# A hybrid decoder step on one core: four tiles' rows turned by VectorE instead of TensorE, and one fold of GLA's first chunk moved ahead

## The chip, the cores and the metric

The kernel runs on one core of one Trainium2 chip. The metric is the device time of one launch in microseconds, the median of several runs. The core has five engines that run side by side, each through its own instructions in order: TensorE (PE in the profile; its weight loads are PEld), VectorE (DVE), ScalarE (ACT), GpSimd (POOL) and SyncE (SP, which issues nearly all DMAs). They wait for each other by semaphores.

## The reference

One inference step of one layer. 2048 prompt tokens and 64 sampled tokens (8 sequences of 8) go through a mixer with two head groups, an output projection, and a squared-ReLU MLP, each with an RMSNorm before and after and a residual:

```python
h = rms_norm(x, g_mix_pre)
proj = h @ w_in                      # split into q, k, v and the GLA parts
attn = sliding-window attention with sinks (window 128)
o    = gated linear attention (GLA), chunked, then rms_norm and silu gate
mix = concat(attn, gla_out) @ w_out
x = x + rms_norm(mix, g_mix_post)
h = rms_norm(x, g_ffn_pre)
u = relu(h @ w_up)
f = (u * u) @ w_down
x = x + rms_norm(f, g_ffn_post)
```

All is f32. The model width is 1024, the MLP's 4096. The new keys, values and GLA states are returned as well.

## The kernel before, in words

The prompt's 2048 rows are 16 tiles of 128 (0 to 15), the 64 sampled rows are tile 16 (`NB`). f32 products are made as three products of split operands: a high part (a ScalarE copy into a rounded type) and a low part (a VectorE subtraction). The stages follow each other: input projection and attention, GLA, the out stage, then the MLP in two halves of 1024 rows (`sb` 0 and 1), each an up stage and a down stage. The MLP's products use a seven-product scheme over 2x2 blocks (Strassen's), so the normalized rows of a tile and of its partner four tiles later (0 and 4, 8 and 12) are combined into seven operands `H[1]` to `H[7]`.

**Out stage.** Tiles go in the order `B_ORDER`: 0, 4, 1, 5, 2, 6, 3, 7, 16, 8, 12, 9, 13, 10, 14, 11, 15. For each tile the 48 products of `out_projecting` (L1581) are issued, and then `residual` of the tile two places earlier in that order. For a tile, `residual` does in steps (a generator; each `yield` ends a step):

- `mixed`: ScalarE squares both halves of the product (`bjunk<-out`, L1696), VectorE adds the sums (`bssq`, L1697), POOL takes the power -0.5 (L221), VectorE scales the product (`x<-out`, L1703; the tile named `x` there is `x1` in the code) and adds the residual (`bx<-x,bx`, L1704).
- ScalarE squares the sum (`bjunk<-bx`, L1809), VectorE and POOL form the factor, VectorE normalizes (`x<-bx,bssq,gpre`, L1812). This is called the tile's norm below.
- PE turns the 128x1024 rows in eight 128x128 transposes into two PSUM banks (`xnT`, L1822), and ScalarE copies each bank into `ht` (L1831), a tile of seven slots. The first of a pair fills slots 0 and 1, the second slots 6 and 2.
- For the second of a pair, VectorE makes the other slots by four subtractions (`ht<-ht`, L1840). Slots 0 and 1 are stored to DRAM after the first tile (L1836), slots 2 to 6 after the second (L1845).

The rows of the next products are loaded by SP (`mt<-mix_d`, L1534) when PE has done the products that used the same buffer, and split by ScalarE (L231) and VectorE (L232). For the last products of the stage the up stage's first operands are split between them (`t`, `H<-hraw`, `s`, recorded at L143, as all that goes through the in-order helper is).

**The second half's rows.** `h_d[1]` holds the seven operands of rows 1024 to 2047. In the first half's down stage `fetch_h` (L1857) loads each operand in two parts (`hraw<-h_d`, 512 KB each), and `load_h` (L1899, L1900) splits it. There the products run in units of 12 (14 with the sampled rows), and their operand pairs (`o0s`, `o0t`, `o1s`, `o1t`, L2253 and L2254) are made two units ahead.

**GLA's first chunk.** `gla(0)` issues its vector work in program order and, at each `yield`, lets a number of steps of other work in. These numbers are `G_FIRST_FILL`. The fill at this place is the projection of the sampled rows (`gproj`, PE), which ends for each column block in a folding of its two halves into `gp_s` (ScalarE copy, VectorE add). The fourth number stands ahead of the six `weighted_queries` (`XQ<-dec,qz`), the fifth behind them. PE can take the next column block only when the fold has emptied its bank.

The build orders each engine's instructions by a compile-time scheduler, which follows program order loosely; so an edit also moves neighbours.

Of the kernel before, what the change touches and what calls it, by code (L numbers as in the profile page):

```python
# [12 lines left out]
F32 = mybir.dt.float32  # L13
F32R = mybir.dt.float32r
U8 = mybir.dt.uint8
AF = mybir.ActivationFunctionType
# [5 lines left out]
P = 128  # L22
# [24 lines left out]
NSB = 2  # L47
# [27 lines left out]
G_ORDER = (0, 1, 2, 3)  # L75
G_FILL = (3, 5, 6, 10, 8, 2, 14, 4, 4, 10, 8, 20)
G_LAST_FILL = (2, 4, 5, 7, 6, 2, 11, 2, 3, 7, 6, 15)
G_FIRST_FILL = (6, 6, 6, 10, 10, 4, 16, 4, 4, 5, 5, 20)
S_WAIT = (2, 6)
WO_PARTS = ((), (0, 1, 2), (3, 4, 5), (6, 7))  # L80
B_ORDER = (*(j + b for j in range(4) for b in (0, 4)), NB, *(j + b for j in range(4) for b in (8, 12)))
# [72 lines left out]
def hybrid_step_kernel(ctx: ExitStack, tc: tile.TileContext, I, O):  # L154
# [1636 lines left out]
    with tc.issue_after(placing[0].ins):  # L1791
        res_x[B_ORDER[1]], loaded = load_x(B_ORDER[1])

    late_copies, latest_store = [], []

    def residual(i, banks, tensor=nc.tensor, scalar=nc.scalar, vector=nc.vector):

        n = rows(i)
        x = res_x.pop(i, None) or load_x(i)[0]
        ssq = sp.tile([P, 48], F32, tag="ssq", name=f"bssq_{i}", bufs=2)  # L1800
        junk = sp.tile([P, D], mybir.dt.bfloat16, tag="junk", name=f"bjunk_{i}", bufs=1)
        x1 = R["x"].tile([P, D], F32, tag="x1", name=f"x1_{i}", bufs=2)
        if i == NB:
            banks = [folded(x1[:NS, c * 512 : (c + 1) * 512], p_) for c, p_ in enumerate(banks)]
        if banks:
            g = g_mix if tensor is nc.tensor else [gpost[:, c * 512 : (c + 1) * 512] for c in range(2)]
            yield from mixed(i, banks, x, x1, junk, ssq, g, sp, scalar, vector)
        rs = ssq[:, 3:5]
        scalar.activation(junk[:n], x[:n], AF.Square, accum_out=ssq[:n, 2:3])  # L1809
        yield  # L1810
        rsqrt_mean(sp, rs[:n, 1:2], ssq[:n, 2:3], n, D, vector=vector)
        vector.scalar_tensor_tensor(x1[:n], x[:n], rs[:n, 1:2], gpre[:n], op0=ALU.mult, op1=ALU.mult)  # L1812
        yield
        sb, j, second = i // 8, i % 4, i % 8 >= 4
        q = slice(j * P, (j + 1) * P)
        if i < NB and not second and i:
            sums[sb, j] = sums[sb, j - 1] if sb and j else ht_place(f"ht_{i}")
        for h in range(2):
            kk = slice(h * 4, h * 4 + 4)
            pt = (bank([P, 512], "ce"[h], f"xnT_{i}_{h}") if te is tensor else next_bank("cdce", f"xnT_{i}_{h}")).rearrange("p (k t) -> p k t", k=4)  # L1820
            for k in range(4):
                tensor.transpose(pt[:, k, :n], x1[:n, (h * 4 + k) * P : (h * 4 + k + 1) * P], ident[:n, :n])  # L1822
            if i == NB:
                split_copy(xsT[:, kk, :NS], xsT[:, kk, NS:], pt[:, :, :NS], vector)
                continue
            ht = sums[sb, j]
            copy = (ht[:, (6, 2)[h] if second else h], pt, AF.Copy)
            if i == B_ORDER[-2]:
                late_copies.append(copy)
            else:  # L1830
                scalar.activation(*copy)  # L1831
# [6 lines left out]
        yield  # L1838
        for out, a, b in ((4, 6, 0), (6, 2, 6), (5, 2, 4), (3, 1, 5)):
            vector.tensor_tensor(ht[:, out], ht[:, a], ht[:, b], op=ALU.subtract)  # L1840
            if out == 6 and i == B_ORDER[-1]:
                yield
        if i == B_ORDER[-3]:
            yield
        latest_store[:] = [nc.sync.dma_start(h_d[sb][:, 2:, :, q], ht[:, 2:])]  # L1845

    h_raws = {}

    def fetch_h(sb, p, home="h"):
        h_raws[p] = []  # L1850
        for k in range(0, KT // 2, 2):
            if isinstance(home, tuple):
# [4 lines left out]
            fetched = nc.sync.dma_start(raw, h_d[sb][:, p - 1, k : k + 2])  # L1857
# [62 lines left out]
    for n, i in enumerate(B_ORDER[2:]):  # L1920
# [227 lines left out]
    def opening(p, taken, ahead, add):  # L2148

        if p == 1:  # L2150
            for copy in late_copies:
                ac.activation(*copy)
            nc.sync.dma_start(h_d[1][:, :2, :, 3 * P :], sums[1, 3][:, :2])
            taken(p)
            next(last_rows)
            loaded = placing[0]
# [473 lines left out]
```

## Time and profile before

| what | value |
|---|---|
| median of 3 runs | 2136.56 us (2136.18 to 2137.39) |
| profiled execution | 2138.09 us, its span 2136.3 us |
| granted TensorE clock | 0.999 of full speed |
| DMA | 421.73 MB, 197 GB/s on average |

The profiled execution is one run by itself, 1.5 us above the median. Its span is the time from the first to the last instruction. In rows by time the columns are start (us from the span's start), length (us), engine, line of the kernel, operation, result and sources, partitions x elements, and count; a bracket gives idle time of the engine just before and what ended it. Several like instructions in one row overlap a little, so start to start is shorter than the sum of their lengths.

### The profile page before, as it was taken

What the parts mean: (1) busy time and instruction counts of PE and PEld (TensorE: products, weight loads), DVE (VectorE), ACT (ScalarE), POOL (GpSimd) and SP (SyncE); (2) the same over time, 40 slices, a digit from 0 to 9 for tenths busy, and PEclk for the clock granted to TensorE, in tenths of its full rate; (3) what the DMA queues carried; (4) which work ended last, traced back from release to release, by engine and by line L of the source; (5) the groups of instructions that cost most, each with busy time, mean ns of one, the idle gap of its engine ahead of it and who ended that gap; (6) DMA issues with size and microseconds to landing.
All of it is one profiled execution on the core that took longest, in us unless ns stands there. A gap on an engine that the chain in (4) does not pass through costs nothing.

```text
span 2136.3 us, 34547 instructions
## 1 busy us (share of the span) xinstructions
PE 2124.3 (99%) x11828; PEld 1839.5 (86%) x11828; DVE 1528.0 (72%) x3209; ACT 1209.9 (57%) x2690; POOL 223.0 (10%) x393
## 2 busy tenths in 40 slices
PE   9999999999999999999999999999999999999998
PEld 9999999999998888888888888888888888888887
DVE  7999878788886667888887655557766666555576
ACT  7999867566764445655554644344454444544454
POOL 4676510000001110000000000000000000000000
PEclk9999999999999999999999999999999999999999
DMA  7444334546667668687876777668544443766685
GB/s 244 150 148 142 113 100 93 128 113 166 189 201 265 202 208 269 223 274 260 277 257 230 262 236 223 209 197 281 185 149 158 157 158 134 253 204 197 190 273 179
DMA packets 309324, 421.73 MB, mean 197 GB/s; under 512 B 80204, under 2 KB 213308, under 8 KB 305036
## 3 DMA queue, kind: packets, MB, share of 16 engines
q1 hardware_dynamic: 308988, 419.26, 61.2%
q8 instruction: 93, 1.52, 0.3%
q14 instruction: 83, 0.68, 0.1%
q10 hardware_dynamic: 160, 0.27, 0.0%
HBM read 270.34 MB, written 148.57 MB: 196 GB/s over the span
## 4 chain that ended last, share of the span: by engine, by line
PE 95%; ACT 2%; DVE 2%; DMA 1%; issue 0%; POOL 0%; DVEq 0%; SPq 0%; ACTq 0%; POOLq 0%
PE dn L143 28%; PE gproj L143 12%; PE uc L143 8%; PE uX L143 8%; PE out L1581 7%; PE proj L143 6%; PE ud L143 4%; PE ue L143 4%; PE ub L143 4%; PE sam L143 2%; PE dsam L143 1%; PE sc L143 1%; PE pT L143 1%; PE av L143 1%; PE out L143 1%; PE xT L143 1%
## 5 line engine op out<-in xcount | busy, mean ns | idle before, releaser
L143 PE MATMUL dn<-o0t,o0s 128*128 128x512 f32 x888 | 345.5, 389 | 0.5 <-DVE f L2268 0.3
L143 PE MATMUL dn<-o0t,o1s 128*128 128x512 f32 x888 | 345.6, 389 | 0.0
L143 PE MATMUL dn<-o1t,o0s 128*128 128x512 f32 x888 | 345.6, 389 | 0.0
L2254 DVE TENSOR_TENSOR o1s<-rs,o0s 128x512 fp32r<-128x512 f32 x224 | 154.7, 691 | 223.3 <-ACT o0s L2253 221.0
L2253 ACT ACTIVATE o0s<-rs 128x512 fp32r<-128x512 f32 x224 | 141.1, 631 | 295.0 <-PE dn L143 261.5
L143 PE MATMUL gproj<-wg,gxh 128*128 128x384 f32 x1024 | 269.7, 341 | 0.0
L143 ACT ACTIVATE st<-st 128x512 f32<-128x512 f32 x224 | 141.1, 630 | 103.9 <-DVE st L143 99.0
L143 PEld LDWEIGHTS dn<-o0t,o0s 128*128 128x128 f32 x888 | 166.8, 188 | 37.2 <-DVE f L2268 1.1
L143 PEld LDWEIGHTS dn<-o1t,o0s 128*128 128x128 f32 x888 | 166.7, 188 | 35.1
L143 PEld LDWEIGHTS dn<-o0t,o1s 128*128 128x128 f32 x888 | 166.7, 188 | 35.0
L143 PE MATMUL gproj<-wg,gxl 128*128 128x384 f32 x576 | 186.4, 341 | 1.7 <-DVE gp_s L143 1.6
L143 PE MATMUL uc<-H,s 128*128 128x512 f32 x768 | 186.5, 391 | 0.0
L143 PEld LDWEIGHTS gproj<-wg,gxh 128*128 128x128 f32 x1024 | 184.3, 188 | 2.5 <-issue 2.1
L143 PE MATMUL uX<-H,w 128*128 128x512 f32 x768 | 185.2, 390 | 0.0
L143 PEld LDWEIGHTS uX<-H,w 128*128 128x128 f32 x768 | 144.0, 188 | 30.3
L143 PEld LDWEIGHTS uc<-H,s 128*128 128x128 f32 x768 | 143.0, 188 | 30.6 <-ACT st L143 0.2
L1581 PE MATMUL out<-wo,mt 128*128 128x512 f32 x680 | 158.8, 392 | 0.4 <-DVE x L1703 0.3
L2254 DVE TENSOR_TENSOR o1t<-rt,o0t 128x512 fp32r<-128x512 f32 x222 | 152.2, 686 | 4.2 <-ACT o0t L2253 4.1
L1581 PEld LDWEIGHTS out<-wo,mt 128*128 128x128 f32 x680 | 126.4, 188 | 27.0 <-issue 1.0
L2253 ACT ACTIVATE o0t<-rt 128x512 fp32r<-128x512 f32 x222 | 136.9, 618 | 9.0 <-DMA rt<-t_d 7.1
L221 POOL TENSOR_TENSOR frs<-rs_v,half 128x1 f32<-128x1 f32 (+1 forms) x13 | 11.5, 891 | 1197.8 <-DVE rs_v L219 1197.8
L143 DVE TENSOR_TENSOR st<-st 128x512 f32<-128x512 f32 x160 | 110.6, 691 | 29.5 <-ACT st L143 25.2
(451 smaller groups left out, 4238.8 us busy)
## 6 DMA issues: line engine op xcount, KB each, us to landing
s_d<-st SPq DMA_DIRECT2D x32, 1792.0 KB
rs<-s_d SPq DMA_DIRECT2D x224, 256.0 KB
raw<-in_w_up SPq DMA_DIRECT2D x64, 512.0 KB
rt<-t_d SPq DMA_DIRECT2D x128, 256.0 KB
rt<-in_w_down SPq DMA_DIRECT2D x96, 256.0 KB
t<-in_w_down SPq DMA_DIRECT2D x64, 256.0 KB
t_d<-t SPq DMA_DIRECT2D x32, 512.0 KB
h_d<-ht SPq DMA_DIRECT2D x8, 1280.0 KB
```

Source lines behind the costliest of these rows:

```text
L143: ins = call(*a, **k)
L221: return nc.gpsimd.tensor_tensor(out, v[:n], e, op=ALU.pow)
L1581: te.matmul(banks[c], x, w[:, c * 512 : (c + 1) * 512], start=k + u == 0, stop=k == KT - 1 and u == n - 1,)
L2253: high = nc.scalar.activation(hi, raw, AF.Copy)
L2254: low = nc.vector.tensor_tensor(lo, raw, f32(hi), op=ALU.subtract)
```

## The change

Two edits.

1. For the prompt tiles 8, 9, 12 and 13, the rows are no longer turned by PE and copied by ScalarE. VectorE turns each half (128x512) in 32x32 blocks straight into `ht`. A 32x32 block transpose leaves each token group of 32 on its own partitions, so the layout of `ht` and of `h_d[1]` changes to blocks for the whole second half: the stores of these four tiles become four DMAs of 32 partitions each, the tiles that PE still turns (10, 11, 14, 15) are copied into the block layout, and `fetch_h` and `load_h` read it in runs of 128 elements. The turned tile's remaining steps (transposes, subtractions, store) are issued one tile behind its norm.
2. In `G_FIRST_FILL` three steps move from the fifth number to the fourth.

```diff
-G_FIRST_FILL = (6, 6, 6, 10, 10, 4, 16, 4, 4, 5, 5, 20)
+G_FIRST_FILL = (6, 6, 6, 13, 7, 4, 16, 4, 4, 5, 5, 20)
...
-    h_d = [dpool.tile([P, 7, KT // 2, BT], F32, name=f"h_d{sb}") for sb in range(NSB)]
+    h_d = [dpool.tile(s, F32, name=f"h_d{sb}") for sb, s in enumerate(([P, 7, KT // 2, BT], [P, 4, 4, 7, P]))]
...
+    def by_blocks(ht):
+        return ht.rearrange("p u k t -> p (u k t)").rearrange("p (b u k x) -> p b u k x", b=4, u=7, k=4)
+
+    def store_blocks(j, us):
+
+        ht, dst = by_blocks(sums[1, j]), h_d[1][:, j]
+        if j > 1:
+            return nc.sync.dma_start(dst[:, :, us], ht[:, :, us].rearrange("p b u k x -> p b u (k x)"))
+        for c in range(4):
+            src = ht[c * 32 : c * 32 + 32, :, us].rearrange("t a u k x -> t a (u k x)")
+            stored = nc.sync.dma_start(dst[:, c, us].rearrange("(a t) u e -> t a (u e)", a=4), src)
+        return stored
...
         for h in range(2):
             kk = slice(h * 4, h * 4 + 4)
+            u = (6, 2)[h] if second else h
+            if 8 <= i < NB and j < 2:
+                vector.transpose(
+                    by_blocks(sums[sb, j])[:, :, u].rearrange("t a k x -> t k a x"),
+                    x1[:, h * 512 : (h + 1) * 512].rearrange("x (k a t) -> x k a t", k=4, a=4),
+                )
+                continue
...
-            copy = (ht[:, (6, 2)[h] if second else h], pt, AF.Copy)
+            out = ht[:, u]
+            if sb:
+                out = by_blocks(ht)[:, :, u].rearrange("p c k x -> p k c x")
+                pt = pt.rearrange("p k (c x) -> p k c x", c=4)
+            copy = (out, pt, AF.Copy)
...
-                nc.sync.dma_start(h_d[sb][:, :2, :, q], ht[:, :2])
+                store_blocks(j, slice(2))
...
-        latest_store[:] = [nc.sync.dma_start(h_d[sb][:, 2:, :, q], ht[:, 2:])]
+        latest_store[:] = [store_blocks(j, slice(2, 7)) if sb else nc.sync.dma_start(h_d[0][:, 2:, :, q], ht[:, 2:])]
...
-            fetched = nc.sync.dma_start(raw, h_d[sb][:, p - 1, k : k + 2])
+            if sb:
+                raw = raw.rearrange("p b t -> p (b t)").rearrange("p (m e) -> p m e", e=P)
+            src = h_d[1][:, k : k + 2, :, p - 1].rearrange("p j c e -> p (j c) e") if sb else h_d[0][:, p - 1, k : k + 2]
+            fetched = nc.sync.dma_start(raw, src)
...
-            split_by(scalar, vector, *(t[:, 2 * n : 2 * n + 2] for t in H[p]), raw)
+            parts = [t[:, 2 * n : 2 * n + 2] for t in H[p]]
+            if sb:
+                parts = [t[:, :, n * 256 : n * 256 + 256].rearrange("p k (m x) -> p m k x", x=32) for t in H[p]]
+                raw = raw.rearrange("p m (k x) -> p m k x", k=4)
+            split_by(scalar, vector, *parts, raw)
...
         elif n > 1:
-            run(residual(*early.pop(0)))
+            blocks_next = 8 <= early[0][0] < NB and early[0][0] % 4 < 2
+            turned_rows.append(residual(*early.pop(0)))
+            if blocks_next:
+                run(turned_rows[-1], 3)
+                run(turned_rows.pop(0) if len(turned_rows) > 1 else ())
+            else:
+                while turned_rows:
+                    run(turned_rows.pop(0))
```

The order of instructions shows it at three places. Numbers at the end of a name tell buffers apart; the lines are those of each kernel.

PE in the out stage before, between the products of tile 9 (`mt_10535`) and those of tile 13 (`mt_10625`), where tile 8's rows are turned:

```order
L1581 MATMUL out_1_10566<-wo_3_9386,mt_10535 128x512
L1581 MATMUL out_1_10566<-wo_3_9385,mt_10535 128x512
L1822 MATMUL xnT_0_10612<-ident,x_8_10595 128x128 x4
L1822 MATMUL xnT_1_10618<-ident,x_8_10595 128x128 x4
L1581 MATMUL out_0_10631<-wo_1_9218,mt_10625 128x512
L1581 MATMUL out_0_10631<-wo_1_9219,mt_10625 128x512
```

PE at the same place now (tile 13's mix rows are `mt_10611`):

```order
L1581 MATMUL out_1_10566<-wo_3_9386,mt_10535 128x512
L1581 MATMUL out_1_10566<-wo_3_9385,mt_10535 128x512
L1581 MATMUL out_0_10617<-wo_1_9218,mt_10611 128x512
L1581 MATMUL out_0_10617<-wo_1_9219,mt_10611 128x512
L1581 MATMUL out_0_10617<-wo_1_9218,mt_10611 128x512 x2
```

The eight transposes are gone; tiles 12, 9 and 13 read alike. At the stage's end the eight of tile 11 stand behind seven products of the up stage, where they stood ahead of all of them.

ScalarE near the end of the stage before: the square of tile 14's rows (`bx_11037`), then of tile 11's product, then the copies of tile 10 (`xnT_0_10994`):

```order
L231 ACTIVATE mt_11007<-mt_11007 128x512
L1809 ACTIVATE bjunk_11040,bssq_11039<-bx_11037 128x1024
L1696 ACTIVATE bjunk_11100,bssq_11099<-out_0_10924 128x512
L1696 ACTIVATE bjunk_11100,bssq_11099<-out_1_10949 128x512
L1831 ACTIVATE ht_10611<-xnT_0_10994 128x512
L1831 ACTIVATE ht_10611<-xnT_1_11000 128x512
```

And now (tile 14's rows are `bx_11009`, tile 11's product `out_0_10886`, tile 10's bank `xnT_0_10966`):

```order
L1696 ACTIVATE bjunk_11012,bssq_11011<-out_1_10811 128x512
L1855 ACTIVATE ht_10687<-xnT_0_10966 128x4x4x32
L1855 ACTIVATE ht_10687<-xnT_1_10972 128x4x4x32
L1822 ACTIVATE bjunk_11012,bssq_11011<-bx_11009 128x1024
L1696 ACTIVATE bjunk_11072,bssq_11071<-out_0_10886 128x512
L1696 ACTIVATE bjunk_11072,bssq_11071<-out_1_10911 128x512
```

The copies, which wait for PE, moved ahead of the square. On VectorE a little later, before (tile 11's norm first, then sums `t`, splits `H` and subtractions `ht` of tile 14):

```order
L1812 SCALAR_TENSOR_TENSOR x_11_11101<-bx_11097,bssq_11099,gpre 128x1024
L143 TENSOR_TENSOR t_0_0_11170<-raw_0_0_10900,raw_0_0_10901 128x4x128
L143 TENSOR_TENSOR t_0_0_11170<-raw_0_0_10900 128x4x128
L143 TENSOR_TENSOR H_0_11174<-hraw_5_0_10914,H_0_11173 128x1024
L1840 TENSOR_TENSOR ht_10611<-ht_10611 128x512
L143 TENSOR_TENSOR H_0_11174<-hraw_5_2_10916,H_0_11173 128x1024
L1840 TENSOR_TENSOR ht_10611<-ht_10611 128x512 x2
L143 TENSOR_TENSOR s_0_0_11180<-t_0_0_11170,s_0_0_11179 128x1024
L1840 TENSOR_TENSOR ht_10611<-ht_10611 128x512
```

And now:

```order
L143 TENSOR_TENSOR t_0_0_11142<-raw_0_0_10862,raw_0_0_10863 128x4x128
L143 TENSOR_TENSOR t_0_0_11142<-raw_0_0_10862 128x4x128
L1866 TENSOR_TENSOR ht_10687<-ht_10687 128x4x128
L143 TENSOR_TENSOR H_0_11146<-hraw_5_0_10876,H_0_11145 128x1024
L1866 TENSOR_TENSOR ht_10687<-ht_10687 128x4x128 x2
L219 TENSOR_SCALAR rs_v<-bssq_11071 128x1
L143 TENSOR_TENSOR H_0_11146<-hraw_5_2_10878,H_0_11145 128x1024
L1866 TENSOR_TENSOR ht_10687<-ht_10687 128x4x128
L1825 SCALAR_TENSOR_TENSOR x_11_11073<-bx_11069,bssq_11071,gpre 128x1024
L143 TENSOR_TENSOR s_0_0_11152<-t_0_0_11142,s_0_0_11151 128x1024
```

Tile 11's norm moved from ahead of that block to its end. In GLA's first chunk VectorE's order differs by one row:

```order
 L143 TENSOR_TENSOR XK<-dec_5020,qkT_5023 128x8x16
 L143 TENSOR_TENSOR XK<-dec_5020,qkT_5023 128x4x32
+L143 SCALAR_TENSOR_TENSOR gp_s<-gproj_0_5133,rstd_all,gp_s 64x384
 L143 TENSOR_TENSOR XQ<-dec_5020,qz 128x256 x6
-L143 SCALAR_TENSOR_TENSOR gp_s<-gproj_0_5133,rstd_all,gp_s 64x384
 L143 TENSOR_TENSOR XK<-dec_5020,qkT_5023 128x2x64
 L143 TENSOR_TENSOR XQ<-dec_5020,qz 128x256
```

The fold of the sampled rows stands ahead of the six weighted queries.

More of the change, by code (lines that the diff above doesn't have):

```diff
@@ L1792, in hybrid_step_kernel @@
         res_x[B_ORDER[1]], loaded = load_x(B_ORDER[1])
-    late_copies, latest_store = [], []
+    late_copies, latest_store, turned_rows = [], [], []
+    def by_blocks(ht):
[8 more added lines that the diff above has]
+        return stored
     def residual(i, banks, tensor=nc.tensor, scalar=nc.scalar, vector=nc.vector):
@@ L1835, in residual @@
             if i < NB and sb and i != B_ORDER[-2]:
-                nc.sync.dma_start(h_d[sb][:, :2, :, q], ht[:, :2])
+                store_blocks(j, slice(2))
             return
         yield
+        ht = sums[sb, j]
+        t = by_blocks(ht).rearrange("p b u k x -> p u b (k x)") if sb else ht
         for out, a, b in ((4, 6, 0), (6, 2, 6), (5, 2, 4), (3, 1, 5)):
-            vector.tensor_tensor(ht[:, out], ht[:, a], ht[:, b], op=ALU.subtract)
+            vector.tensor_tensor(t[:, out], t[:, a], t[:, b], op=ALU.subtract)
             if out == 6 and i == B_ORDER[-1]:
@@ L2152, in opening @@
                 ac.activation(*copy)
-            nc.sync.dma_start(h_d[1][:, :2, :, 3 * P :], sums[1, 3][:, :2])
+            store_blocks(3, slice(2))
             taken(p)
```

## The prediction

> **What bounds the kernel now.** I read the page's busy times first, then who waited for whom, then the order in time of TensorE and VectorE around the two edited places.
>
> ```profile
> PE 2124.3 (99%) x11828; PEld 1839.5 (86%) x11828; DVE 1528.0 (72%) x3209; ACT 1209.9 (57%) x2690; POOL 223.0 (10%) x393
> ```
>
> TensorE (PE) is busy 99% of the span, so time can come only from PE instructions that go away and from the few places where PE waits. The longest of PE's waits in the list of waits (total, times, longest) is this one:
>
> ```profile
> PE gproj L143 <- DVE gp_s L143: 1.6, 1, 1.6
> ```
>
> It is one wait. VectorE's fold that ends it is over at 322.3 us (row further down), so it began at 320.7; the second edit moves that fold. In the out stage PE's order in time reads (start, length, engine, instruction):
>
> ```profile
> 777.03 1.03 PE L1822 MATMUL xnT<-ident,x 128*128 128x128 f32 x8
> 777.82 11.18 PE L1581 MATMUL out<-wo,mt 128*128 128x512 f32 x48
> 788.84 1.03 PE L1822 MATMUL xnT<-ident,x 128*128 128x128 f32 x8
> ...
> 824.26 1.03 PE L1822 MATMUL xnT<-ident,x 128*128 128x128 f32 x8
> ...
> 830.63 1.03 PE L1822 MATMUL xnT<-ident,x 128*128 128x128 f32 x8
> ...
> 836.99 1.03 PE L1822 MATMUL xnT<-ident,x 128*128 128x128 f32 x8
> ```
>
> Eight transposes (tile 8 at 777.03, tile 12 at 788.84, tiles 10, 14 and 11 at 824.26, 830.63 and 836.99), then the 48 products of a later tile, with no gap.
>
> **Removed: 32 transposes on PE.** Tiles 8, 12, 9 and 13 lose 8 each. The price of 8 is start to start: 777.82 - 777.03 = 0.79 us, since the next product starts before the last transpose ends. 4 x 0.79 = 3.16 us off PE. The row of the tile gives another figure:
>
> ```profile
> L1822 PE MATMUL xnT<-ident,x x128: 222/272/332, 675.1 to 837.8; 128*128 128x128 f32 x120, 64*128 64x64 f32 x8
> ```
>
> One instruction lasts 272 ns at the median, but they overlap: 0.79 / 8 = 99 ns each. I take 99. [...]
>
> **Added: 8 VectorE transposes; removed: 8 ScalarE copies.** The same form stands in the GLA stage (busy, mean ns):
>
> ```profile
> L143 DVE STREAM_TRANSPOSE turned<-og 128x512 f32<-128x512 f32 x14 | 9.9, 706 | 0.0
> ```
>
> 8 x 0.71 = 5.6 us more on VectorE (DVE). The stage and what follows it (busy of PE, PEld, DVE, ACT, POOL):
>
> ```profile
> 775.00:845.00 70.00, 70.00 (x344) 58.62 (x343) 45.40 (x70) 33.16 (x67) 6.49 (x12) 1.00 0.73 236
> 845.00:860.00 15.00, 15.00 (x73) 12.36 (x73) 14.20 (x18) 11.67 (x16) 0.54 (x1) 1.00 0.92 297
> ```
>
> DVE has 24.6 us idle in the first 70 us, which covers 5.6; but from 845 on it has 0.8 us idle in 15, so whatever DVE is late by at the stage's end is not made up and PE waits for it. That end is the place that decides.
>
> **The stage's tail.** Nothing of the tiles 8, 12, 9, 13 makes PE wait by my walk through the new order: each one's split of the next mix tile on DVE ends about 1 us or more ahead of its products. It is tile 10, the first that PE still turns, where order matters. ScalarE (ACT) now stands with tile 10's two copies from PSUM ahead of the square of tile 14's rows; before, that square was first. So tile 14's norm waits for PE's transposes of tile 10, and tile 11's norm, which DVE now does after a block of up-stage splits, comes behind it. The durations (ACT, then DVE):
>
> ```profile
> 820.11 1.06 ACT L1809 ACTIVATE bjunk<-bx 128x1024 bf16<-128x1024 f32 x1 [3.55 <-DVE bx L1704]
> ...
> 831.26 1.09 ACT L1831 ACTIVATE ht<-xnT 128x512 f32<-128x512 f32 x2
> ```
>
> ```profile
> 822.11 1.28 DVE L1812 SCALAR_TENSOR_TENSOR x<-bx,bssq,gpre 128x1024 f32<-128x1024 f32 x1 [0.66 <-POOL bssq L221]
> 825.18 0.16 DVE L1697 TENSOR_TENSOR bssq<-bssq 128x1 f32<-128x1 f32 x1 [1.79 <-ACT bjunk L1696]
> ...
> 826.27 1.41 DVE L1703 SCALAR_TENSOR_TENSOR x<-out,bssq,wo 128x512 f32<-128x512 f32 x2 [0.74 <-POOL bssq L221]
> 827.72 1.23 DVE L1704 TENSOR_TENSOR bx<-x,bx 128x1024 f32<-128x1024 f32 x1
> ...
> 831.03 1.28 DVE L1812 SCALAR_TENSOR_TENSOR x<-bx,bssq,gpre 128x1024 f32<-128x1024 f32 x1 [0.66 <-POOL bssq L221]
> 832.23 0.69 DVE L143 TENSOR_TENSOR t<-raw,raw 128x512 f32<-128x512 f32 x1
> ...
> 836.31 1.29 DVE L1840 TENSOR_TENSOR ht<-ht 128x512 f32<-128x512 f32 x2
> 837.51 1.22 DVE L143 TENSOR_TENSOR s<-t,s 128x1024 fp32r<-128x1024 f32 x1
> ```
>
> Transposes of tile 10 start at 824.26 - 3.16 = 821.10. Copies start 0.6 later (for tile 14, 831.26 against 830.63) and take 1.09: 822.8. From the square's start to the norm's is 822.11 - 820.11 = 2.0: norm of tile 14 at 824.8, over at 826.0 (1.2, as 831.03 to 832.23). Then tile 11: sums of squares to scaling 1.09 (825.18 to 826.27), scaling 1.45 (826.27 to 827.72), residual add 1.15 (1.23 less the 0.08 by which such rows overlap the next): 829.7. Then the block that was behind the norm and now is ahead of it: 832.23 to 837.51 is 5.28, plus one subtraction of 0.6 (two take 837.51 - 836.31 = 1.2) and 0.15: 835.75. The norm itself 1.28: 837.0. PE wants tile 11's rows 836.99 - 824.26 = 12.73 after tile 10's, plus seven products of the up stage that now stand ahead (7 x 0.23 = 1.6, with 0.23 from 48 products in 11.02 us): 821.10 + 14.33 = 835.4. So PE waits 1.6 us there, and the 3.16 shrinks to 1.56.
>
> Behind it DVE runs the old sequence, without one subtraction (it moved ahead): its row at 837.51 starts at 836.95, and the rest is 0.56 + 0.6 = 1.15 us earlier than before. The next meeting:
>
> ```profile
> 850.89 2.35 DVE L143 TENSOR_TENSOR H<-hraw,H 128x1024 fp32r<-128x1024 f32 x2
> ```
>
> ```profile
> 851.85 3.10 PE L143 MATMUL ua<-H,s 128*128 128x512 f32 x12
> ```
>
> The second of these products needs the first of the two splits, over at 850.89 + 1.17 = 852.06, and starts at 851.85 + 0.23 = 852.08: no slack. PE, 1.56 early, meets DVE, 1.15 early, and loses 0.4. Out stage: -1.15. Bounds: -3.16 if the tail costs nothing; about +1 if a load of tile 10's rows, now issued behind four stores, is 3 us later than I have it.
>
> [...]
>
> **Moved: GLA's first fills.** Three fill steps move ahead of the first weighted queries, and DVE has the first sampled folding ahead of the six queries:
>
> ```profile
> 319.21 0.58 ACT L143 ACTIVATE gp_s<-gproj,rstd_all 64x384 f32<-64x384 f32 x1
> ```
>
> ```profile
> 319.68 2.10 DVE L143 TENSOR_TENSOR XQ<-dec,qz 128x256 f32<-128x256 f32 x6
> 321.69 0.61 DVE L143 SCALAR_TENSOR_TENSOR gp_s<-gproj,rstd_all,gp_s 64x384 f32<-64x384 f32 x1
> ...
> 323.11 0.61 DVE L143 SCALAR_TENSOR_TENSOR gp_s<-gproj,rstd_all,gp_s 64x384 f32<-64x384 f32 x1 [0.28 <-ACT gp_s L143]
> ```
>
> ACT's half is over at 319.79, so DVE can fold by 320.45 instead of 322.30, before PE runs dry at 320.7: all 1.6 goes. The queries end 0.6 later, still 6 us ahead of their use. The second folding stays at 323.11 and ends at 323.72; PE, now early, reaches its bank at about 323.7, which can give 0.1 back. I take -1.5; bounds 0 and -1.6.
>
> **Stores and fetches.** The 4 stores of those tiles become 16 on SP (0.3 to 0.4 us each). They wait for DVE, with loads of mix tiles behind them; by my walk these still issue as PE frees their buffers. The fetches of the second half's operands change from one 4 KB run to eight of 512 B per partition. One such fetch (issue, then ACT's wait, then the operand pair behind it):
>
> ```profile
> 1241.34 0.42 SPq L1857 DMA_DIRECT2D hraw<-h_d  x1
> ```
>
> ```profile
> 1242.18 0.63 ACT L2253 ACTIVATE o0s<-rs 128x512 fp32r<-128x512 f32 x1 [2.06 <-PE dn L143]
> ...
> 1246.53 1.06 ACT L1899 ACTIVATE H<-hraw 128x1024 fp32r<-128x1024 f32 x1 [3.19 <-DMA hraw<-h_d]
> ```
>
> ```profile
> 1249.36 0.69 DVE L2254 TENSOR_TENSOR o1t<-rt,o0t 128x512 fp32r<-128x512 f32 x1
> ```
>
> It takes 5.2 us. The pair behind it, due at 1242.18 + 3.2 (14 products of 0.23) = 1245.4, is ready at 1250.05 and needed two units of 3.2 later, 1251.8: cover 1.8 us. Time per byte (last columns DMA share, GB/s), 512 B stores against mostly 4 KB loads:
>
> ```profile
> 820.00:824.00 4.00, 4.00 (x19) 3.33 (x18) 1.46 (x3) 1.84 (x4) 0.54 (x1) 1.00 0.98 292
> 830.00:834.00 4.00, 4.00 (x23) 3.40 (x22) 3.12 (x5) 3.61 (x7) 0.54 (x1) 1.00 1.08 386
> ```
>
> 292 / 0.98 against 386 / 1.08 is 1.2 times as long: 1.0 us on 5.2, under the cover. Cost 0, bounds 0 and 1 us for each of the seven operands fetched so. The splits' strided form I cost at nothing: they are as many elements per partition.
>
> **Sum.** -1.15 - 1.5 = -2.65 us. The profiled execution took 2138.09 (span 2136.3), 1.5 above the median 2136.56; as a difference, 2133.9 on the median. 0.2% is 4.3 us, about what a measurement of this kernel can tell from no change, so this counts as no change.
>
> **Rivals.**
> - *No wait in the tail* (ACT's square of tile 14 comes in time, or PE's order gives DVE room): -3.16 - 1.5 = 2131.9. For it: DVE's 24.6 us idle; against: the chain above. 15%.
> - *A tighter tail* (tile 10's load late, tile 15's products held by PSUM banks that tile 14's scaling frees): out stage 0 to +1, so 2135.1 to 2136.1. 17%.
> - *GLA gives nothing back* (the fold waits on ACT, or attention weights of tile 0 become the wait): -1.15 alone, 2135.4. 10%.
> - *Slower: fetches in 512 B runs.* If one takes twice its 5.2 us, PE waits 5.2 - 1.8 = 3.4 for each of the seven: 23.8 - 2.65, 2157.7. It decides (2.65 + 4.3 = 6.95 us lost) from 5.2 + 1.8 + 6.95 / 7 = 8.0 us a fetch. The 1.2 above speaks against. 5%.
> - *Transposes cost their busy time* (8.7 us by 272 ns): 2126.4. Against: start to start. 3%.
>
> Forecast 50%. Faster by over 0.2% (under 2132.3): most of the first rival, and the last: 13%. Slower: 5%. Same: 82%. Range 2131.6 to 2137.0: from the first rival to the second with its bounds and spread of the runs.
>
> **What would show it.** PE's wait for gp_s gone; 32 fewer transposes; the products of tiles 13, 10, 14 and 11 one behind the other 11.02 us apart; a PE wait of 1 to 2 us on x in front of tile 11's transposes; no PE wait at 1190 to 1355 on operands. Wrong if that wait is absent (faster) or if PE waits on operands behind fetches (slower).

## The result and the profile after

| | median | runs | profiled execution |
|---|---|---|---|
| before, on the same chip | 2137.38 us | 2136.14 to 2140.37 | 2138.09 us, span 2136.3 |
| changed | 2141.14 us | 2137.56 to 2144.53 | 2138.12 us, span 2136.3 |

The ratio is 1.0016, 95% interval [1.0009, 1.0023]: 3.8 us (0.18%) more, where 2.65 us less was forecast. It lies outside the range and on the other side. The profiled execution is one of the shorter of the changed kernel, so some 3 us of its median are not in the trace below. The granted clock of these 20 runs is 0.997 to 0.999, 0.9985 on average; in the runs of the kernel before that were made beside the experiments it is 0.9994 to 0.9996 on average. A difference of 0.001 over the span is 2 us, an estimate, so a slower TensorE clock can be a part of the loss.

The page's busy times: 32 PE instructions fewer and 3.4 us less of PE, 5 us more of DVE, in the same span.

```profile
PE 2120.9 (99%) x11796; PEld 1836.1 (86%) x11796; DVE 1532.9 (72%) x3217; ACT 1206.6 (56%) x2682; POOL 225.6 (11%) x393
```

What PE waits for (total, times, longest). The wait for `gp_s` went from 1.6 to 0.2; four others are new or longer, three of them in the out stage; the fourth (`dn`) is taken up under The fetches.

```profile
PE xnT L1842 <- DVE x L1825: 3.5, 2, 2.9
PE dn L143 <- ACT f L2411: 1.5, 1, 1.5
...
PE xnT L1842 <- DVE bssq L1697: 0.9, 1, 0.9
PE out L1581 <- ACT ht L1855: 0.7, 1, 0.7
...
PE gproj L143 <- DVE gp_s L143: 0.2, 1, 0.2
```

PE's order in time through the same stretch as before: tile 16's transposes, then 240 products (tiles 9, 13, 10, 14, 11) without a gap, then tile 10's transposes, tile 15's first 24 products, tile 14's transposes, and so on.

```profile
761.74 0.71 PE L1842 MATMUL xnT<-ident,x 64*128 64x64 f32 x8
762.38 54.70 PE L1581 MATMUL out<-wo,mt 128*128 128x512 f32 x240
817.95 1.06 PE L1842 MATMUL xnT<-ident,x 128*128 128x128 f32 x8 [0.87 <-DVE bssq L1697]
819.70 5.70 PE L1581 MATMUL out<-wo,mt 128*128 128x512 f32 x24 [0.69 <-ACT ht L1855]
...
836.33 1.07 PE L1842 MATMUL xnT<-ident,x 128*128 128x128 f32 x8 [2.94 <-DVE x L1825]
837.15 2.05 PE L143 MATMUL uX<-H,w 128*128 128x512 f32 x5
839.00 1.91 PE L143 MATMUL sam<-w,xsT 128*128 128x256 f32 x8
840.71 3.09 PE L143 MATMUL uX<-H,w 128*128 128x512 f32 x12
843.63 1.12 PE L143 MATMUL sam<-w,xsT 128*128 128x256 f32 x8
...
851.13 1.17 PE L143 MATMUL ua<-H,s 128*128 128x512 f32 x4
```

The 32 transposes are gone at the price foreseen or a little more: from tile 16's transposes to the idle time before tile 10's it is 817.08 - 761.74 = 55.3 us, 824.26 - 765.38 = 58.9 before. Then 0.87 + 0.69 + 2.94 = 4.5 us of waiting, where 2.0 was forecast. After the last wait PE is also slow: five `uX` take 839.00 - 837.15 = 1.85 us (1.15 at 0.23 each), eight `sam` 1.71 (0.96 at 843.63). That is 1.5 us more. The stretches (PE busy, granted clock, DMA share, GB/s) show the clock:

```profile
834.00:836.00 2.00, 0.00 (x0) 1.00 1.04 410
836.00:838.00 2.00, 1.67 (x11) 0.92 0.99 336
838.00:840.00 2.00, 2.00 (x8) 0.50 0.99 293
840.00:842.00 2.00, 2.00 (x10) 0.73 1.07 402
842.00:844.00 2.00, 2.00 (x12) 1.00 1.03 399
```

Why the waits: on SP's queue (start, length, engine) tile 10's rows, tile 15's mix and tile 14's rows are loaded behind tile 13's last four block stores.

```profile
797.46 0.49 SPq L1534 DMA_DIRECT2D mt<-mix_d  x1
803.58 3.50 SPq L1806 DMA_DIRECT2D h_d<-ht  x4
807.18 1.50 SPq L1784 DMA_DIRECT2D bx<-in_x_prompt  x1
808.78 1.25 SPq L1534 DMA_DIRECT2D mt<-mix_d  x1
810.13 0.46 SPq L1784 DMA_DIRECT2D bx<-in_x_prompt  x1
```

From 797.95 to 803.58 the queue stands: its next instruction, the first of the four stores, waits for VectorE's last subtraction of tile 13 (802.87 to 803.55). Tile 10's rows, which in the kernel before were issued at 789.08, stand behind it and go out at 807.18. DVE has waited 7.6 us for them when it adds them; tile 10's norm is over at 817.80, when PE has been idle since 817.08, and tile 11's, last in the chain, starts at 834.90:

```profile
813.01 1.23 DVE L1704 TENSOR_TENSOR bx<-x,bx 128x1024 f32<-128x1024 f32 x1 [7.60 <-DMA bx<-in_x_prompt]
...
816.52 1.28 DVE L1825 SCALAR_TENSOR_TENSOR x<-bx,bssq,gpre 128x1024 f32<-128x1024 f32 x1 [0.66 <-POOL bssq L221]
...
834.90 1.28 DVE L1825 SCALAR_TENSOR_TENSOR x<-bx,bssq,gpre 128x1024 f32<-128x1024 f32 x1 [0.44 <-POOL bssq L221]
```

And the stores themselves are slow. DMA share and GB/s (last two columns) while such stores alone run, in the changed kernel:

```profile
805.00:807.00 2.00, 1.00 0.95 201
```

and while one store of a whole tile (128 partitions, 512 B runs) runs in the kernel before:

```profile
798.00:801.00 3.00, 1.00 0.98 290
```

The four move 4 x 320 KB = 1.31 MB; at 201 GB/s that is 6.5 us of the DMA engines, against 4.5 us at 290.

### The profile page after: what moved, and what is told of

Same layout as the page of the kernel before. It is cut to its first block, busy times and chain, and to the rows that moved or that the text cites. A ratio compares the mean times of both kernels' runs of the same rounds, so it can differ in the third digit from the quotient of the medians.

```text
span 2136.3 us, 34496 instructions
## 1 busy us (share of the span) xinstructions
PE 2120.9 (99%) x11796; PEld 1836.1 (86%) x11796; DVE 1532.9 (72%) x3217; ACT 1206.6 (56%) x2682; POOL 225.6 (11%) x393
## 4 chain that ended last, share of the span: by engine, by line
PE 91%; DMA 3%; DVE 2%; ACT 2%; SPq 1%; issue 1%; POOL 0%; DVEq 0%; ACTq 0%; POOLq 0%
PE dn L143 28%; PE gproj L143 12%; PE uc L143 8%; PE uX L143 8%; PE proj L143 6%; PE out L1581 4%; PE ud L143 4%; PE ue L143 4%; PE ub L143 4%; PE sam L143 2%; PE dsam L143 1%; PE sc L143 1%; PE pT L143 1%; PE av L143 1%; DMA mt<-mix_d 1%; PE gl L143 1%
```

## The experiments

Each ratio is against runs of the kernel before on the same chip. To see where a run's time went, three lengths are taken from the rows of PE's tiles: GLA from its first to its last `gproj`, the out stage from the first `xnT` to the first `ua`, the rest from there to the last `dn`.

```
kernel            ratio  95% interval       GLA    out    rest
before            1                         372.7  176.8  1278.1
changed           1.0016 [1.0009, 1.0023]   370.6  179.4  1278.6
gla_only          0.9997 [0.9988, 1.0005]   370.8  177.8  1279.7
layout_only       1.0004 [0.9995, 1.0013]   372.5  176.5  1278.9
two_tiles         0.9990 [0.9981, 0.9999]   370.8  176.7  1277.3
load_early        1.0035 [1.0022, 1.0047]   370.9  183.5  1280.8
hoist             1.0022 [1.0013, 1.0031]   370.8  181.1  1278.7
stores_act        1.0010 [1.0001, 1.0018]   370.8  177.3  1282.6
no_lag13          1.0008 [0.9999, 1.0017]   371.0  178.0  1281.8
no_lag            1.0066 [1.0053, 1.0078]   370.9  191.3  1278.2
two_queues        0.9979 [0.9970, 0.9989]   371.0  172.9  1279.0
two_queues_b      0.9980 [0.9971, 0.9988]   370.6  173.3  1279.3
after_4k          1.0008 [0.9999, 1.0017]   370.7  179.7  1278.3
two_4k            0.9992 [0.9983, 1.0000]   370.9  176.1  1278.2
two_4k_q2         0.9982 [0.9973, 0.9991]   370.8  175.0  1277.5
last4_act         0.9996 [0.9987, 1.0005]   370.8  176.4  1280.8
load_early_act    1.0011 [1.0003, 1.0020]   370.9  178.4  1282.9
q2_4k             0.9980 [0.9971, 0.9989]   370.9  173.4  1282.4
q2_halves         0.9976 [0.9966, 0.9985]   370.8  173.5  1278.6
q2_no_gla         0.9990 [0.9981, 0.9999]   372.6  172.8  1278.9
```

The theories: loads late behind the block stores; the fetches in 512 B runs; the GLA edit giving nothing; the order of ScalarE and VectorE in the tail.

### The parts by themselves

**gla_only**, the kernel before with one line changed:

```diff
-G_FIRST_FILL = (6, 6, 6, 10, 10, 4, 16, 4, 4, 5, 5, 20)
+G_FIRST_FILL = (6, 6, 6, 13, 7, 4, 16, 4, 4, 5, 5, 20)
```

> The kernel before with the second edit alone (fill numbers 13, 7 in GLA's first chunk). If the fold's move is worth what the trace of the changed kernel shows there (PE's wait for gp_s 0.2 us instead of 1.6), the time is about 1.4 us under the kernel before's, ratio 0.9993 to 0.9994. If the edit gives nothing or what it gives is lost later, 1.0000; if it is what cost the 3.8 us, 1.0016.

0.9997, its interval reaching from 0.9988 to 1.0005: by time alone undecided. The trace decides: PE's wait is the same 0.2 us, and GLA is 370.6 to 371.0 us long in all 17 profiles with the edit, 372.5 to 372.7 in the three without. The edit gives 1.5 to 2.1 us.

**layout_only**, the new arrangement of the second half's rows without block transposes:

```diff
-            if 8 <= i < NB and j < 2:
...
-                continue
...
-        if j > 1:
+        if j >= 0:
```

(in `store_blocks`, so that every tile is stored by 128 partitions; no lag, GLA as before)

> The kernel before with the new arrangement in DRAM alone: the second half's sums stored and fetched as in the changed kernel, in 512 B runs on the fetch, with TensorE turning every tile, no lag, and GLA as before. Theory 'fetches': the 14 fetches are longer, one or more of them past their cover, so PE waits 1.5 us or more on operands in the down stage, and the runs spread: +1.5 to +5 us, ratio 1.0007 to 1.0023. Theory 'late load' (tile 10's rows behind the block stores cost the time): no such stores here, ratio 0.9998 to 1.0003.

1.0004 [0.9995, 1.0013], between the two cases: the fetches cost 2.8 us at most, and the out stage is as before. The side result is the rate of a store of 128 partitions in runs of 2.5 KB, double that of the block stores, whose runs are as long:

```profile
798.00:799.00 1.00, 1.00 0.99 399
```

**two_tiles**, only tiles 8 and 12 turned by VectorE:

```diff
-            if 8 <= i < NB and j < 2:
+            if 8 <= i < NB and j < 1:
...
-            blocks_next = 8 <= early[0][0] < NB and early[0][0] % 4 < 2
+            blocks_next = 8 <= early[0][0] < NB and early[0][0] % 4 < 1
```

> The changed kernel with only tiles 8 and 12 turned by VectorE; tiles 9 and 13 are turned by TensorE, without the lag from tile 9 on. Theory 'late load': 16 transposes fewer (-1.6 us), a tail as before's, GLA -1.4: 3.0 us under the kernel before, ratio 0.9986. Theory 'fetches': the same less 1.5 to 5 us of waits in the down stage, ratio 0.9993 to 1.0009.

0.9990, between the two cases: faster than before, with the same fetches as the changed kernel. So what costs is in tiles 9 and 13 and what follows them. Of the 16 transposes' 1.6 us, 1.26 are given back at one place, in ScalarE's order: its split of tile 14's mix stands behind tile 9's two copies from PSUM.

```profile
797.84 11.19 PE L1581 MATMUL out<-wo,mt 128*128 128x512 f32 x48 [1.26 <-ACT mt L231]
```

### Loads ahead of the stores

**load_early**, tile 10's load issued before tile 13's last stores:

```diff
+            if turned_rows and not blocks_next:
+                res_x[early[0][0]] = load_x(early[0][0])[0]
             turned_rows.append(residual(*early.pop(0)))
```

> The changed kernel with one move: the load of tile 10's rows is issued ahead of tile 13's last four block stores. Theory 'late load': PE's waits around tiles 10, 15 and 11 (0.9, 0.7 and 2.9 us) shrink to the 1.6 us of the prediction, the granted clock stays at 1.00 there, and the time falls by 3 to 4 us against the changed kernel's, to a ratio of about 1.0000. Theory 'fetches': the tail gets shorter but the runs stay at 1.0010 or more, since the down stage's waits are as they were.

Worse, 1.0035. The scheduler put tile 15's mix load behind tile 10's own store, which waits for ScalarE's copies of PE's transposes (SP's queue, then PE):

```profile
820.14 0.38 SPq L1803 DMA_DIRECT2D h_d<-ht  x1
820.62 0.46 SPq L1534 DMA_DIRECT2D mt<-mix_d  x1
```

```profile
826.03 7.56 PE L1581 MATMUL out<-wo,mt 128*128 128x512 f32 x24 [6.60 <-ACT mt L231]
```

The expectation failed as written. Tile 10's rows, issued at 799.58, no longer make PE wait; but one load behind one waiting store costs 6.6 us: the mechanism, at another load.

**hoist** moves tile 15's mix as well:

```diff
             if turned_rows and not blocks_next:
+                mixes[B_ORDER[-1]] = load_mix(B_ORDER[-1])
                 res_x[early[0][0]] = load_x(early[0][0])[0]
```

> The changed kernel with two loads, tile 10's rows and tile 15's mix, issued ahead of tile 13's last four block stores. The run with tile 10's load alone moved had tile 15's mix load behind a store that waits for TensorE (6.6 us of PE waiting); this one should not have that wait. Theory 'loads behind the stores': tile 10's and 15's waits go, ratio 0.9990 to 1.0005, unless tile 14's rows, whose load now stands behind tile 10's store, take over as the late ones (then 1.0015 or more). Theory 'fetches': 1.0010 or more with no wait of the tail left.

The 6.6 us are gone, and the case named as "unless" came: tile 14's rows are now behind tile 10's store. PE waits 2.5 us at 834.29 for tile 14's transposes, and the clock falls to 0.50 behind it. Moving single loads only moves the wait.

**stores_act**, all 16 block stores on ScalarE's queue:

```diff
-            stored = nc.sync.dma_start(dst[:, c, us].rearrange("(a t) u e -> t a (u e)", a=4), src)
+            stored = nc.scalar.dma_start(dst[:, c, us].rearrange("(a t) u e -> t a (u e)", a=4), src)
```

> The changed kernel with the 16 block stores issued on ScalarE's queue instead of SyncE's, so that no load stands behind them. Theory 'loads behind the stores on one queue': PE waits for no x and no mix tile in the out stage beyond the 1.6 us of the prediction before tile 11, the granted clock stays 1.00, and the time is 2134 to 2136 us, ratio 0.9985 to 0.9995, less whatever the stores hold up on ScalarE. Theory 'fetches in 512 B runs': about 1 us better than the changed kernel, ratio 1.0010 or more, with the wait in the down stage near 1277 us. Theory 'the tail's order on ScalarE and VectorE' (nothing to do with loads): ratio 1.0010 to 1.0016 with PE waiting for x in front of tile 11's transposes as in the changed kernel (2.9 us).

The out stage is 2.1 us shorter than the changed kernel's, with no slow clock, but PE waits 1.5 us at 797 for a bank: ScalarE waits 9.2 us, to 793, for a mix tile, and the squares that lead to the bank's release stand behind that split. The median (1.0010) does not show the gain. By it the case foreseen for the fetches has come, and the trace agrees: the rest is long, 1282.6, with a wait of 1.67 us at 1276 and a slow clock behind it (see The fetches).

**last4_act** moves tile 13's last four alone:

```diff
+            queue = nc.scalar if j == 1 and us.start else nc.sync
-            stored = nc.sync.dma_start(dst[:, c, us].rearrange("(a t) u e -> t a (u e)", a=4), src)
+            stored = queue.dma_start(dst[:, c, us].rearrange("(a t) u e -> t a (u e)", a=4), src)
```

> The changed kernel with four stores alone (tile 13's last ones, the four ahead of tile 10's load on SyncE's queue) issued on ScalarE's queue. Theory 'loads behind these four stores': tile 10's and 14's rows and tile 15's mix are issued some 4 us earlier, PE's waits for tile 10, for the banks of tile 14 and for tile 11 (0.9, 0.7, 2.9 us) go or fall under 1 us together, clock 1.00: ratio 0.9980 to 0.9992. Theory 'all 16 stores weigh on the DMA engines': at most 1 us better than the changed kernel, 1.0010 to 1.0016.

0.9996: 4 us under the changed kernel's ratio, though short of what was expected. PE's waits in the out stage are now these, 2.3 us instead of 4.5, and the clock stays at 1.00; the 1.06 in front of tile 11 and the 0.46 in front of `ua` are the prediction's own two waits (1.6 and 0.4):

```profile
809.77 10.28 PE L1581 MATMUL out<-wo,mt 128*128 128x512 f32 x44 [0.82 <-DVE mt L232]
834.99 1.07 PE L1843 MATMUL xnT<-ident,x 128*128 128x128 f32 x8 [1.06 <-DVE x L1826]
849.93 2.32 PE L143 MATMUL ua<-H,s 128*128 128x512 f32 x9 [0.46 <-DVE H L143]
```

**load_early_act**, load_early with tile 10's first store on ScalarE's queue:

```diff
+            queue = nc.scalar if j == 2 and not us.start else nc.sync
-            return nc.sync.dma_start(dst[:, :, us], ht[:, :, us].rearrange("p b u k x -> p b u (k x)"))
+            return queue.dma_start(dst[:, :, us], ht[:, :, us].rearrange("p b u k x -> p b u (k x)"))
```

> The run with tile 10's load moved ahead, with one store more off the queue: tile 10's first one, which waits for TensorE's transposes, is issued on ScalarE's queue, so that tile 15's mix load does not wait behind it. Theory 'loads behind stores': the 6.6 us wait for that mix tile goes, and if tile 10's rows were what came late first, the three waits of the changed kernel go too: 0.9980 to 0.9995. If tile 10's rows were not the cause (tile 14's, whose load still stands behind the four stores, are), 1.0008 to 1.0016.

1.0011, the second case: tile 15's mix and tile 14's rows still stand behind the four stores, and PE waits 1.8 us for the mix and 2.6 for tile 11. Tile 10's load alone is not enough.

### The lag

**no_lag13** turns tile 13 at once:

```diff
                 run(turned_rows.pop(0) if len(turned_rows) > 1 else ())
+                if i == B_ORDER[-3]:
+                    run(turned_rows.pop())
```

> The changed kernel with tile 13 turned at once instead of one tile later. If the lag of the last block tile is what makes the tail late, its subtractions and stores move ahead and the ratio falls to 0.9990 to 1.0000; if the queue of block stores is (their number is unchanged), 1.0010 to 1.0020.

1.0008, inside neither case. The scheduler makes nearly the same order of it, with the same three waits (0.9, 0.7, 2.9 us), so it told nothing about the lag. **no_lag** drops it everywhere:

```diff
-            blocks_next = 8 <= early[0][0] < NB and early[0][0] % 4 < 2
+            blocks_next = False
```

> The changed kernel without the lag: each tile's rows are turned straight behind their normalization, as before, by VectorE for tiles 8, 12, 9 and 13. If the lag is what costs, ratio 0.9985 to 0.9995 (three us less than the kernel before); if the 16 stores on one queue or the fetches are, 1.0005 to 1.0020, about as the changed kernel.

1.0066 and an out stage of 191.3 us: far off what was expected. Without the lag the transposes and subtractions (774.20 to 778.05) stand ahead of the next mix split on VectorE, and PE waits 2.54 us for that split, later 1.88 us for another (`out <- DVE mt`), with a slow clock behind both. In this order of work the lag is needed.

### Two queues

**two_queues** divides each four stores between SP and ScalarE (repeated as two_queues_b):

```diff
-            stored = nc.sync.dma_start(dst[:, c, us].rearrange("(a t) u e -> t a (u e)", a=4), src)
+            stored = (nc.sync, nc.scalar)[c % 2].dma_start(dst[:, c, us].rearrange("(a t) u e -> t a (u e)", a=4), src)
```

> The changed kernel with its block stores divided between two queues: two of each four (token blocks 0 and 2) on SyncE, two (1 and 3) on ScalarE. In the changed kernel these stores, 32 partitions each, move 200 GB/s at a DMA share of 0.94 to 0.96. If 32 partitions at a time are the limit, two stores side by side move 300 to 400 GB/s, each tile's last stores are over in about 4 us instead of 6.5, tile 10's rows arrive earlier and the out stage gets 2 us shorter: ratio 1.0000 to 1.0010. If the limit is in the writes themselves, still 200 GB/s, and 1.0010 to 1.0020.

> The run with the block stores on two queues once more, the best so far (0.9979 [0.9970, 0.9989]): if that holds, 0.9975 to 0.9985 again, with the out stage's end some 4 us earlier against its start than in the kernel before.

0.9979 and 0.9980: 4.5 us under the kernel before, better than either case expected of the first (the repeat came as expected), and for another reason than the one given there. The rate of two such stores side by side is still

```profile
781.00:783.00 2.00, 1.00 0.91 195
```

But with half as many stores on SP, the loads of tiles 10 and 14 are issued ahead of tile 13's last ones, 15 and 13 us earlier than in the changed kernel:

```profile
791.96 0.38 SPq L1784 DMA_DIRECT2D bx<-in_x_prompt  x1
...
797.07 0.33 SPq L1784 DMA_DIRECT2D bx<-in_x_prompt  x1
...
801.00 3.40 SPq L1806 DMA_DIRECT2D h_d<-ht  x2
```

Tile 10's norm is at 806.73 instead of 816.52, tile 11's comes ahead of the up stage's block on VectorE again, and PE has no gap from tile 8 to `ua`:

```profile
806.73 1.28 DVE L1825 SCALAR_TENSOR_TENSOR x<-bx,bssq,gpre 128x1024 f32<-128x1024 f32 x1 [0.66 <-POOL bssq L221]
```

**q2_halves** pairs other partitions: `c // 2` in place of `c % 2`, so 0 to 31 run beside 64 to 95, not beside 32 to 63.

> The run with two queues, but with the blocks of partitions 0 to 63 on SyncE's queue and those of 64 to 127 on ScalarE's, so that at a time a store from the lower half of the partitions runs beside one from the upper half (with two queues so far, 0 to 31 ran beside 32 to 63). If it is the way from the partitions that limits (a store of 128 partitions moved 400 GB/s, one of 32 200), the stores move 300 to 400 GB/s in tile 12's, 9's and 13's store windows; if it is 200 again, something else limits them. Either way the time is that of the run with two queues, 0.9975 to 0.9985, since PE no longer waits for these stores.

0.9976, the lowest, though its interval holds two_queues too. The same two stores, with no other transfer issued on SP from 776.6 to 783.4, now move

```profile
781.00:782.50 1.50, 1.00 0.99 353
```

So a second queue alone did not raise the rate (195, against 201 of the stores on one queue), and a store from partitions 64 apart beside the first did (353). By the test set before this run that speaks for the way from the partitions as the limit of a block store; why the first pair gets no more than one queue's stores and the second does is not shown. The kernel's time did not change with it (0.9976 against 0.9979 and 0.9980).

**q2_no_gla** is two_queues with the old fill numbers.

> The run with two queues without the second edit: 32 transposes fewer alone. If all 3.2 us of them come through, 0.9983 to 0.9988, with the GLA stage as long as before (372.5 us from its first to its last projection, against 370.6 to 371 with the edit); if the out stage's gain hangs on GLA's, 0.9990 or more.

0.9990 is by number the edge of the second case, with an interval that reaches into the first. The trace decides: the median is 2.8 us under before's, the out stage 4.0 us shorter, GLA 372.6 as foreseen. So the out stage's 3.2 us come through without GLA's edit.

### The fetches

**after_4k** keeps tiles 10, 14, 11 and 15 in DRAM as before, so half of the fetches are in 4 KB runs:

```diff
-            src = h_d[1][:, k : k + 2, :, p - 1].rearrange("p j c e -> p (j c) e") if sb else h_d[0][:, p - 1, k : k + 2]
+            if not sb:
+                src = h_d[0][:, p - 1, k : k + 2]
+            elif k:
+                src = h_d[2][:, p - 1].rearrange("p j (c e) -> p (j c) e", c=4)
+            else:
+                src = h_d[1][:, :, :, p - 1].rearrange("p j c e -> p (j c) e")
```

> The changed kernel with the two token tiles of each column that TensorE turns (10, 14 and 11, 15) kept in DRAM as before, so that half of the second half's fetches come in 4 KB runs again (the other half stay in 512 B runs). Theory 'fetches': the down stage's waits on operands near 1277 us and beside it, 1 to 3 us, go at least by half: 1 to 2 us under the changed kernel, ratio 1.0005 to 1.0012. Theory 'the tail alone': 1.0016 as the changed kernel, or worse by the stores of these tiles, which go back to 512 B pieces of the fetch's 4 KB.

**two_4k** does the same to two_tiles (all but tiles 8 and 12 in long runs), **two_4k_q2** adds the second queue, **q2_4k** is after_4k with it.

> Tiles 8 and 12 alone turned by VectorE (the run with two tiles), and all but their own rows kept in DRAM in long runs: a quarter of the fetched bytes in 512 B runs, a quarter in 2 KB, half in 4 KB. Theory 'fetches': 0.5 to 1.5 us under the run with two tiles (ratio 0.9990 to the kernel before), so 0.9983 to 0.9988. Theory 'the fetches cost nothing': 0.9990 again.

> As the run before, with the block stores divided between SyncE's and ScalarE's queues. If 32 partitions at a time are the limit of these stores, the mix loads behind them land earlier and the remaining 1.3 us wait for a mix tile near 797 us in the run with two tiles goes: 0.9978 to 0.9985. If that wait is of ScalarE's order and not of the stores, no change against the run without the second queue.

> Block stores on two queues, and the second half's tiles that TensorE turns kept in DRAM as before, so that half of the fetches are in 4 KB runs. If the fetches in 512 B runs cost 1 us or more in the down stage, 0.5 to 1 us under the run with two queues (0.9974 to 0.9977); if they cost nothing that can be measured, the same as it.

after_4k 1.0008 against 1.0016, two_4k 0.9992 against two_tiles' 0.9990, q2_4k 0.9980 against 0.9980: no difference that the intervals allow to be named. With the second queue two_4k_q2 (0.9982) no longer has the 1.3 us wait for tile 14's mix that two_tiles and two_4k have: there ScalarE splits that mix (792.36) ahead of tile 9's copies (798.02).

The traces tell more. One fetch of the down stage is late, and PE waits behind it for a bank that ScalarE empties (`f<-dn`) only after it has split the fetched operand. In the changed kernel:

```profile
1266.04 0.42 SPq L1886 DMA_DIRECT2D hraw<-h_d  x1
...
1272.76 1.06 ACT L1932 ACTIVATE H<-hraw 128x1024 fp32r<-128x1024 f32 x1 [4.70 <-DMA hraw<-h_d]
...
1276.90 0.60 ACT L2411 ACTIVATE f<-dn 128x512 f32<-128x512 f32 x1
...
1277.55 0.50 PE L143 MATMUL dn<-o0t,o0s 128*128 128x512 f32 x1 [1.51 <-ACT f L2411]
```

and in the kernel before:

```profile
1267.03 0.42 SPq L1857 DMA_DIRECT2D hraw<-h_d  x1
...
1272.17 1.06 ACT L1899 ACTIVATE H<-hraw 128x1024 fp32r<-128x1024 f32 x1 [3.13 <-DMA hraw<-h_d]
...
1277.26 0.50 PE L143 MATMUL dn<-o0t,o0s 128*128 128x512 f32 x1 [0.22 <-ACT f L2371]
```

From SP's issue to ScalarE's split this fetch takes 6.72 us, before 5.14. In 13 of the 20 profiles PE's wait here is the fetch's time less 5.2 us, from 0.34 us (two_tiles, 5.53) to 2.46 (load_early_act, 7.66); in the other seven it is 0.2 to 1.1 us. In the six with 1.67 us or more (stores_act, q2_4k, no_lag13, load_early, last4_act, load_early_act) the granted clock falls behind it, as in stores_act:

```profile
1278.00:1280.00 2.00, 2.00 (x6) 0.50 0.80 237
```

The clock is below 1.00 for some 3.4 us there, and 1.7 us are lost each time. From `ua` to the end the profiles range from 1277.3 to 1282.9 us; without PE's waits and this slow clock all lie between 1276.7 and 1277.9. So waits and clock make nearly the whole range.

**Left open.** Why this fetch is late. With all rows in 512 B runs it takes 5.5 us in layout_only and two_tiles, 5.5 to 7.7 in the kernels with four tiles turned. after_4k and q2_4k (6.3 and 6.9) do not settle it, since they keep this fetch, of tiles 8, 12, 9 and 13, in short runs. The 3 us of the changed kernel's median that its trace lacks can be such a fetch with its slow clock; no trace of a longer execution shows it.

## Why the prediction was wrong

1. *Transposes off PE, 3.16 us.* Right: 240 products without a gap, and the whole of it appears once the tail is free (172.8 to 173.5 against 176.8). Start to start was the price, not the 272 ns.
2. *8 VectorE transposes, covered by idle time.* Right with the lag (691 ns each in the trace, 173 for a 128x128 block, against 99 on PE); no_lag shows what they cost ahead of a mix split (PE waits 2.54 us).
3. *The tail, 2.0 us lost.* It was 6.0. The chain was read rightly (tile 10's copies, tile 14's norm, tile 11's norm behind the block; the wait on `x` stood where foreseen), but it began too late: tile 10's transposes waited too (0.87), tile 15's products waited for the banks (0.69), tile 11's wait was 2.94 instead of 1.6, and the clock fell behind it (1.5 us). With loads on time the chain is as read: in last4_act 1.06 in front of tile 11 and 0.46 in front of `ua`.
4. *The step that failed* is in the stores: "The 4 stores of those tiles become 16 on SP (0.3 to 0.4 us each). They wait for DVE, with loads of mix tiles behind them; by my walk these still issue as PE frees their buffers." The stores were priced by their issue, and the loads behind them were taken to go out in time. Four stores made SP's queue stand 5.6 us for VectorE, then held SP 3.5 us and the DMA engines 6.5 us at 201 GB/s. And the loads that mattered were of rows: tile 10's went out at 807.18, before the change at 789.08. With these loads ahead of the stores (two_queues) the three waits and the slow clock are gone, and the out stage is 6.5 us shorter than the changed kernel's.
5. *The bound.* "About +1 if a load of tile 10's rows, now issued behind four stores, is 3 us later than I have it" was the right case, as was the second rival (tile 10's load late, tile 15's products held by banks): 17% and 0 to +1 for the out stage, where it took +2.6. The rival had no slow clock in it.
6. *GLA, -1.5.* Right: 1.5 to 2.1 us between the profiles.
7. *Fetches in 512 B runs, 0, under a cover of 1.8 us.* A second step that failed. The lengthening was put at 1.0 us, and 1.6 was measured at one fetch of the trace; but the cover was read from the operand pair behind the fetch of 1241 us. At the next one, of 1266 us, ScalarE's emptying of a bank stands behind it, and PE waits from 5.2 us on: 1.5 us, where the bound was 1. In six other profiles a slow clock follows. That the 512 B runs alone lengthen it is not shown.

The two traces are equally long, 2136.3 us: 2.65 us of gain are missing, and the out stage alone is 3.75 us off (+2.6 instead of -1.15). The 3.8 us between the medians are not in them. Against two_queues the changed kernel's ratio is 0.0037 higher, 7.9 us, of which the out stage has 6.5 in the traces; the rest is not located.

With the tail free the first rival, 4.66 us under before, is what two_queues and two_queues_b measure: 0.9979 and 0.9980 (4.5 and 4.3 us).

## What to carry to other kernels

Price a store by the time it makes the queue stand until its data are there (5.6 us here for four) and by the time it holds the queue and the DMA engines (3.5 and 6.5 us), not by its issue, and then look at each load behind it in that queue for who waits. A store from 32 partitions ran at half the rate of one from 128 here (201 and 399 GB/s); with such stores on two queues the loads came in time, and with partitions 64 apart side by side most of the rate came back (353 GB/s), without a further gain in time. For the cover of a fetch, look at everything that stands behind it on the engine that takes it in, at each of its places, not at one. When a scheduler sets the queue's order, moving one load by hand moves another behind something that waits: read the order of the whole queue, not of the one load.

## What was not expected of the hardware

- A store from 32 partitions moved 195 to 201 GB/s, one from 128 in equal runs 399; two at a time from 0 to 31 and 32 to 63 still moved 195 together, from 0 to 31 and 64 to 95 353.
- The granted clock fell to 0.50, for some 3.4 us, after PE had been idle for 2.94 us (changed kernel, 1.5 to 1.7 us lost), after 2.48 us in hoist, and in the down stage after 1.67 us (stores_act). It stayed at 1.00 after 2.91 us (no_lag13), 2.60 us (load_early_act) and 1.63 us (two_queues_b). So no length of wait divides the two in these runs.
